# Two transformer blocks in float32: seven products in place of eight in parts of the gate and up layers, with adding DMAs

## The chip, the cores and the metric

One core of a Trainium2 chip runs the whole program. The metric is the device time of one execution in microseconds (us), and lower is better. The kernel before took 2581.62 us, the median of three runs (2581.48 to 2582.09).

## The reference

Two transformer blocks run one after the other on 256 tokens of width 2048, in float32. The first has window attention, gated linear attention and a feed forward layer; the second has latent attention, sparse attention, cross attention and a wide layer. The change is in the first block's feed forward layer, whose width is 5632:

```python
z = rmsnorm(h, norm_ffn_g[l])
ff = (jax.nn.silu(z @ w_ffn_gate[l]) * (z @ w_ffn_up[l])) @ w_ffn_down[l]
h = h + ff.astype(h.dtype)
```

## The kernel before

**Products.** TensorE multiplies in the type float32r, so that each float32 operand is held as the sum of a high part (the value rounded to float32r) and a low part (what is left), and each product of two tiles is three matmuls: high by high, high by low, low by high (`three` in `dense`, line 179, matmuls at L187). The activation's transposed parts (the class `Act`; zT for the gate and up layers, ffT for the down layer) lie in SBUF; they are the stationary operand, 128 rows of the inner dimension by 128 tokens. The weights stream from memory.

**Units.** A weight block of 256 rows by 512 columns, that is two row tiles, is a unit. `emit` (line 224) runs through the list of units. For each it calls `split` on a unit LEAD places ahead, then `load` on one still further ahead, then the unit's own matmuls. `load` issues the DMA into one of RAWB = 6 raw buffers on SP's queue (L232). `split` makes the high part with a ScalarE copy (L246) and the low part with a VectorE subtraction raw - high (L248); in a few units, those marked pool, GpSimd makes the low part. The parts go to LEAD + 1 rotating buffers called whi and wlo, with LEAD = 3. The split of unit n therefore writes buffers that an earlier unit's matmuls have to have finished reading. Each engine works through its instructions in the order in which the program issued them.

```python
nc.scalar.activation(out=hv, in_=r, func=AF.Copy)
eng = nc.gpsimd if u.pool else nc.vector
eng.tensor_tensor(out=l[:, : u.kn, : u.cn], in0=r, in1=hv.bitcast(F32), op=ALU.subtract)
```

**The feed forward layer.** It goes in three parts of 4, 4 and 3 chunks of 512 columns. For each chunk, `dense` puts eight units of the gate's weights into the program and eight of the up's, each unit with 12 matmuls (two row tiles, two token tiles, three matmuls). After the gate's units `evac_gate` (line 852) takes silu from PSUM on ScalarE (L858); after the up's, `evac_up` (line 871) multiplies on VectorE (L877). `ff_tr` transposes the result on TensorE (L289) into ffT one and two units later, with `hilo` splitting it on ScalarE (L277) and VectorE (L278). After each part four chunks of the down product follow, added to the residual by `evac_down` (L885). zT itself is written by `residual` (line 810) during the output product `w_out` before the gate: `make_h1` adds on VectorE (L845), `square_sum` squares on ScalarE (L308), and `to_act` transposes and splits with the gain (L295, L280, L281).

**Memory.** PSUM's eight banks are two accumulators of two banks and four rotating banks for the rest. SBUF is handed out by hand as 12 pages of 8 KB, 8 halves of 4 KB and 8 small pieces a partition.

**The end.** `last_chunk` does one half of the tokens after the other (matmuls at L1352); the parts of its first units are kept in pages, four of its eight with LEAD = 3, and every second low part there is made by GpSimd.

Of the kernel before, what the change touches and what calls it, by code (L numbers as in the profile page):

```python
# [19 lines left out]
LEAD = 3  # L20
RAWB = 6
NPAGE = 12
NHALF = 8
NBIT = 8
# [8 lines left out]
class Act:  # L33
    """A feature-major operand of a product, as the sum of two float32r parts."""
# [18 lines left out]

class Unit:
# [5 lines left out]
    def __init__(self, src, kn, cn, mm, pool=False, keep=False):  # L60
        self.src, self.kn, self.cn, self.mm, self.pool, self.keep = src, kn, cn, mm, pool, keep
# [3 lines left out]
def kernel(  # L65
# [18 lines left out]
    psa = ctx.enter_context(tc.tile_pool(name="psa", bufs=2, space=PS))  # L84
    pss = ctx.enter_context(tc.tile_pool(name="pss", bufs=4, space=PS))
# [10 lines left out]
    def take(lst, pool, name, shape, dt):  # L96
        if not lst:
            raise RuntimeError(f"no room for {name}: {sorted((v[1], v[3]) for v in owner.values())}")
# [8 lines left out]

    def half(name, shape, dt=F32):
        return take(free_h, halves, name, shape, dt) if free_h else page(name, shape, dt)
# [4 lines left out]
    def free(*ts):  # L114
        for t in ts:
            if isinstance(t, Act):
                free(*t.pages)
            else:
                lst, tag = owner.pop(id(t))[:2]
                lst.append(tag)  # L120
# [18 lines left out]

    def bank(name, shape):  # L140
        return pss.tile(shape, F32, tag="ps", name=name)

# [11 lines left out]
    def dense(W, c0, cn, kts, act, jobs, k_off=0, ka=0, src=None, pool=None, first=True, last=True, hold=None, groups=None, evac=None):  # L154
        """Appends the units of act^T-by-W products.

        jobs: ("N", off, n, b) tokens-by-columns products or ("T", off, n, b) columns-by-tokens
        ones, b the bank of the accumulator they go to (None: a bank for each half of the tokens).
        """
        hold = {} if hold is None else hold  # L160
        k0 = 0
        for kn in groups or [KG] * (kts // KG):
# [3 lines left out]
            else:  # L166
                s = src(k0, kn)

            def mm(hi, lo, k0=k0, kn=kn):
                if k0 == 0 and first:  # L170
                    hold["acc"] = psa.tile([P, 2, 512], F32, tag="acc", name="acc")
# [39 lines left out]

    after = {}
# [4 lines left out]
    def sched(u, *steps):  # L217
        """Puts closures behind units: (gap, fn) comes gap units after the one before it."""
# [5 lines left out]
    def emit(start):  # L224
        us = [e for kind, e in prog if kind == "U"]
        raws, spl = {}, {}

        def load(i):
            if i < len(us):
                r = wraw.tile([P, KG, 512], F32, tag="raw", name="raw")  # L230
                for dst, ap in us[i].src:
                    nc.sync.dma_start(dst(r), ap)  # L232
                raws[i] = r

        def split(i):
            if i < len(us):
                u = us[i]
                r = raws.pop(i)[:, : u.kn, : u.cn]
# [6 lines left out]
                hv = h[:, : u.kn, : u.cn]  # L245
                nc.scalar.activation(out=hv, in_=r, func=AF.Copy)  # L246
                eng = nc.gpsimd if u.pool else nc.vector
                eng.tensor_tensor(out=l[:, : u.kn, : u.cn], in0=r, in1=hv.bitcast(F32), op=ALU.subtract)  # L248
                spl[i] = (h, l)

        start(load, split)
        for j in range(LEAD):
            if j > 1:
                split(j)
            load(j + RAWB)
        i = 0
        for kind, e in prog:
# [4 lines left out]
            load(i + LEAD + RAWB)  # L262
# [20 lines left out]
    def to_act(src, dst, k, gain=None):  # L283
        """dst's row tiles k, k+1 from src(t, k), a [tokens, 128] block of half t."""
# [12 lines left out]

    def to_T(src, dst):
        """dst [128, 2, 256] (SBUF) from src(t, a)."""
# [10 lines left out]
    def rstd(ss, n, dst):  # L310
        """dst = (ss / n + eps) ** -0.5"""
# [5 lines left out]
    def bcast_a(r, scale=1.0):  # L317
        """With bcast_b(dst): dst [128, 256] is r ([tokens, 2]) along the free axis, on every partition."""
# [22 lines left out]
    junk = ctx.enter_context(tc.tile_pool(name="junk", bufs=2))  # L341
# [196 lines left out]
    def prep_kva():  # L538
        """Keys and values with the tokens of each half in reverse order."""
# [270 lines left out]
    def residual(name_T, gain, ssname, make):  # L810
        """The closure for chunk j of a residual update: make(j, t, acc) writes h[t]'s columns."""
        def evac(j):
            def fn(acc):
                if j == 0:
                    env[ssname] = small(ssname, [P, 2, 4])
                    env[name_T] = new_act(name_T, 16)
                if "h" not in env:
# [6 lines left out]
                for a in range(2):  # L824
                    k = 4 * j + 2 * a
                    later(2 + a, lambda k=k: to_act(lambda t, kk: h[t][:, kk * P : (kk + 1) * P], env[name_T], k, gain))
# [22 lines left out]
    res_h1 = residual("zT", G_FFN, "ssh1", make_h1)  # L849
# [742 lines left out]
```

## Time and profile before

| what | value |
|---|---|
| runs | 2581.48, 2581.62, 2582.09 us (median 2581.62) |
| profiled execution, first to last instruction (span) | 2579.6 us; no other time is listed for it |
| TensorE busy | 2561.9 us (99%) in 12464 instructions |
| VectorE busy | 1435.2 us (56%) |
| ScalarE busy | 1175.3 us (46%) |
| GpSimd busy | 65.7 us (3%) |
| mean granted TensorE clock | 0.999 |

In the profile, PE is TensorE's matmuls, PEld its weight loads, DVE VectorE, ACT ScalarE, POOL GpSimd and SP the engine that issues most DMAs. A busy time is what an engine spent inside instructions. Matmuls are pipelined, so that two of them overlap in the records, and the step from one to the next is the number that counts. The idle time of an engine has behind it in brackets what ended it. L187 is line 187 of the kernel.

### The profile page before, as it was taken

Reading aid. Unit: us, or ns where it says so; the run is one execution under the profiler, and the core shown is the slowest. Engines: PE = TensorE matmul, PEld = TensorE weight load, DVE = VectorE, ACT = ScalarE, POOL = GpSimd, SP = SyncE. Lnnn points to the kernel's source line nnn. Section 1 sums busy time; section 2 is a strip of 40 time slices with the busy share of each in tenths; the row PEclk is TensorE's granted clock in tenths of the full one; section 3 lists DMA queues with packets and bytes.
Section 4 is the critical chain, followed back from the end, with each engine's and each line's share of the span. In section 5 each row is a group of like instructions: output and inputs, shape, how many; then the busy total and the mean of one; then the engine's idle time right before and its main releaser. Section 6 shows DMA issues by size and latency. Waiting matters only on the chain.

```text
span 2579.6 us, 32028 instructions
## 1 busy us (share of the span) xinstructions
PE 2561.9 (99%) x12464; PEld 2146.7 (83%) x12464; DVE 1435.2 (56%) x1651; ACT 1175.3 (46%) x1562; POOL 65.7 (3%) x69
## 2 busy tenths in 40 slices
PE   8999999999999999999999999999999999999998
PEld 7898788888888888888889978889888888888886
DVE  5755465555455445555566658565655555455554
ACT  5545344444444344434455444464544443443443
POOL 1000000000000000000000000000100000000002
PEclk9999999999999999999999999999999999999999
DMA  7455566656665666566655734554665656656653
GB/s 254 155 166 173 154 212 189 188 188 187 189 188 193 191 191 190 189 210 190 191 170 170 203 115 151 187 180 139 189 193 189 193 183 193 190 185 209 187 187 129
DMA packets 259544, 472.77 MB, mean 183 GB/s; under 512 B 19402, under 2 KB 48848, under 8 KB 259136
## 3 DMA queue, kind: packets, MB, share of 16 engines
q1 hardware_dynamic: 256816, 461.76, 58.7%
q0 software_dynamic: 2544, 8.96, 1.0%
q8 instruction: 97, 1.59, 0.2%
q14 instruction: 55, 0.45, 0.0%
q10 hardware_dynamic: 32, 0.01, 0.0%
HBM read 468.55 MB, written 2.12 MB: 182 GB/s over the span
## 4 chain that ended last, share of the span: by engine, by line
PE 98%; issue 0%; ACT 0%; DMA 0%; POOL 0%; DVE 0%; SPq 0%; POOLq 0%; ACTq 0%
PE acc L187 92%; PE pt L289 1%; PE pt L295 1%; PE ptr L479 0%; PE po L499 0%; PE sc L1057 0%; PE ptT L303 0%; DMA raw<-in_w_in_dram 0%; PE sc L1056 0%; PE psi L1127 0%; PE sc L566 0%; PE po L494 0%; POOL wlo L248 0%; PE sc L1199 0%; ACT whi L246 0%
## 5 line engine op out<-in xcount | busy, mean ns | idle before, releaser
L248 DVE TENSOR_TENSOR wlo<-raw,whi 128x1024 fp32r<-128x1024 f32 (+5 forms) x889 | 1062.4, 1200 | 826.8 <-ACT whi L246 822.3
L246 ACT ACTIVATE whi<-raw 128x1024 fp32r<-128x1024 f32 (+5 forms) x895 | 921.6, 1033 | 903.6 <-PE acc L187 888.8
L187 PE MATMUL acc<-whi,ffTh 128*128 128x512 f32 x832 | 325.6, 391 | 0.0
L187 PE MATMUL acc<-whi,ffTl 128*128 128x512 f32 x832 | 324.0, 389 | 0.0
L187 PE MATMUL acc<-wlo,ffTh 128*128 128x512 f32 x832 | 323.7, 389 | 0.0
L187 PE MATMUL acc<-whi,zTh 128*128 128x512 f32 x704 | 275.7, 392 | 0.0
L187 PE MATMUL acc<-whi,zTl 128*128 128x512 f32 x704 | 274.2, 389 | 0.0
L187 PE MATMUL acc<-wlo,zTh 128*128 128x512 f32 x704 | 273.9, 389 | 0.0
L187 PE MATMUL acc<-whi,x4Th 128*128 128x512 f32 x512 | 201.9, 394 | 0.0
L187 PE MATMUL acc<-whi,uTh 128*128 128x512 f32 (+2 forms) x512 | 198.9, 388 | 2.4 <-ACT whi L246 1.8
L187 PE MATMUL acc<-whi,x4Tl 128*128 128x512 f32 x512 | 199.7, 390 | 0.0
L187 PE MATMUL acc<-wlo,x4Th 128*128 128x512 f32 x512 | 199.3, 389 | 0.0
L187 PE MATMUL acc<-whi,uTl 128*128 128x512 f32 (+2 forms) x512 | 193.9, 379 | 0.6 <-DVE uTl L281 0.6
L187 PE MATMUL acc<-wlo,uTh 128*128 128x512 f32 (+2 forms) x512 | 193.7, 378 | 0.0
L187 PEld LDWEIGHTS acc<-whi,ffTl 128*128 128x128 f32 x832 | 156.2, 188 | 32.8
L187 PEld LDWEIGHTS acc<-wlo,ffTh 128*128 128x128 f32 x832 | 156.3, 188 | 31.9
L187 PEld LDWEIGHTS acc<-whi,ffTh 128*128 128x128 f32 x832 | 156.2, 188 | 31.8
L187 PEld LDWEIGHTS acc<-whi,zTl 128*128 128x128 f32 x704 | 132.1, 188 | 27.8
L187 PEld LDWEIGHTS acc<-wlo,zTh 128*128 128x128 f32 x704 | 132.2, 188 | 27.0
L187 PEld LDWEIGHTS acc<-whi,zTh 128*128 128x128 f32 x704 | 132.2, 188 | 26.8
L187 PE MATMUL acc<-whi,u2Th 128*128 128x512 f32 (+2 forms) x352 | 132.6, 377 | 0.0
L187 PE MATMUL acc<-whi,u2Tl 128*128 128x512 f32 (+2 forms) x352 | 129.0, 366 | 0.0
(446 smaller groups left out, 3353.9 us busy)
## 6 DMA issues: line engine op xcount, KB each, us to landing
raw<-in_w_in_dram SPq DMA_DIRECT2D x167, 512.0 KB, 4.1
raw<-in_w_up_dram SPq DMA_DIRECT2D x128, 512.0 KB, 3.8
raw<-in_w_down_dram SPq DMA_DIRECT2D x128, 512.0 KB, 4.6
raw<-in_w_ffn_gate_dram SPq DMA_DIRECT2D x88, 512.0 KB, 4.4
raw<-in_w_ffn_up_dram SPq DMA_DIRECT2D x88, 512.0 KB, 3.8
raw<-in_w_ffn_down_dram SPq DMA_DIRECT2D x88, 512.0 KB, 4.2
raw<-in_w_out_dram SPq DMA_DIRECT2D x64, 512.0 KB, 4.3
raw<-in_w_in_dram SPq DMA_DIRECT2D x24, 368.0 KB, 3.3
```

The costliest lines, as they stand in the source:

```text
L187: nc.tensor.matmul(dst, lhsT=v if tr else u, rhs=u if tr else v, start=st, stop=end and j == 2, skip_group_check=True,)
L246: nc.scalar.activation(out=hv, in_=r, func=AF.Copy)
L248: eng.tensor_tensor(out=l[:, : u.kn, : u.cn], in0=r, in1=hv.bitcast(F32), op=ALU.subtract)
L289: nc.tensor.transpose(pt[:, a, t * P : (t + 1) * P], src(t, k + a), ident)
L295: nc.tensor.transpose(pt[:, t * P : (t + 1) * P], src(t, k + a), ident)
```

## The change

**Seven products.** `dense2` takes the gate's and the up's units of a chunk together. With two token tiles (rows), a pair of row tiles of the weights (inner) and gate and up (columns), the product of a pair is a 2 by 2 by 2 block product, eight tile products. In pairs marked S (three of the eight, by `kinds_z = "SCCSCSCC"`) seven products of sums of tiles stand in for the eight; in pairs marked C there are eight, into four of the seven accumulators. Each product is three matmuls as before. An S pair is four units: x (two products), u (two), v (two) and y (one); a C pair is two units of four products each. A chunk is 22 units. The sums of weights are made in `split` by three VectorE instructions of an S pair. The sums of activations are made once, in `to_act_sums`, while zT is written.

**Accumulators.** The seven accumulators take seven of PSUM's eight banks; the eighth holds the transposes meanwhile. `early` reads three of the seven after the third S pair; `finish` reads the other four with five additions at the chunk's end, and then `evac_gu` does silu and the multiplication from SBUF. The transposes follow 4 and 6 units later (3 and 4 in a part's last chunk).

**Adding DMA.** In C pairs that follow a C pair (the third and the eighth of a chunk, four units) VectorE makes no low part: ScalarE writes minus the high part into wlo, and an accumulating DMA on GpSimd's queue adds raw to it.

**Room.** LEAD goes from 3 to 4; two more buffers (wsum) hold sums of weights; halves go from 8 to 6, small pieces from 8 to 5, the buffers of `junk` from 2 to 1. When the halves run out, a page is now cut in two. `load_more` loads as many units ahead as there are raw buffers. The diff's core (the definition of `three` in `dense2` is the same three matmuls):

```diff
-LEAD = 3
+LEAD = 4
-NHALF = 8
-NBIT = 8
+NHALF = 6
+NBIT = 5
...
+    wsum = ctx.enter_context(tc.tile_pool(name="wsum", bufs=2))
...
+    def new_seven():
+        rot[:] = [7]
+        at = {1: 0, 3: 1, 5: 4, 7: 5, 6: 6, 4: 2, 2: 3}
+        return {i: psum.tile([P, 512], F32, tag=f"b{b}", name="acc") for i, b in at.items()}
...
+            if kinds[p] == "S":
+                qd = Quad()
+                fin = p == last_s
+                def mx(hi, lo, p=p, q=q, sm_=sm_, fin=fin):
+                    if p == 0:
+                        begin()
+                    three(1, q(0, 0), (hi[:, 0], lo[:, 0]), fin)
+                    three(3, sm_(3), (hi[:, 1], lo[:, 1]))
+                def mu(hi, lo, sm_=sm_, fin=fin):
+                    three(5, sm_(0), (hi[:, 0], lo[:, 0]))
+                    three(7, sm_(2), (hi[:, 1], lo[:, 1]), fin)
+                def mv(hi, lo, q=q, sm_=sm_, fin=fin):
+                    three(6, sm_(1), (hi[:, 0], lo[:, 0]), fin)
+                    three(4, q(1, 1), (hi[:, 1], lo[:, 1]))
+                    if fin:
+                        hold["c"] = early(hold["g"])
+                def my(hi, lo, q=q):
+                    three(2, q(0, 1), (hi[:, 0], lo[:, 0]))
+                x = [(lambda r: r[:, 0:1], blk(Wb, cb, k)), (lambda r: r[:, 1:2], blk(Wa, ca, k + 1))]
+                y = [(lambda r: r[:, 0:1], blk(Wa, ca, k)), (lambda r: r[:, 1:2], blk(Wb, cb, k + 1))]
+                for src, kn, mm, part in (([x, y], 2, mx, "x"), ([], 2, mu, "u"), ([], 2, mv, "v"), ([], 1, my, "y")):
+                    prog.append(("U", Unit(src, kn, 512, mm, quad=qd, part=part)))
...
+                def ma(hi, lo, q=q, sm_=sm_, end=end):
+                    for i in range(2):
+                        three(5, q(1, i), (hi[:, i], lo[:, i]), end and i == 1)
+                    for i in range(2):
+                        three(3, sm_(i), (hi[:, i], lo[:, i]), end and i == 1)
+                def mb(hi, lo, q=q, end=end):
+                    for i in range(2):
+                        three(2, q(0, i), (hi[:, i], lo[:, i]), end and i == 1)
+                    for i in range(2):
+                        three(4, q(1, i), (hi[:, i], lo[:, i]), end and i == 1)
+                for W, c, mm in ((Wa, ca, ma), (Wb, cb, mb)):
+                    prog.append(("U", Unit([[(lambda r: r, blk(W, c, k, 2))]], 2, 512, mm, add=kinds[p - 1] == "C")))
+        def early(g):
+            c = [half("c0", [P, 2, 512]), half("c1", [P, 2, 512])]
+            nc.scalar.activation(out=c[0][:, 1], in_=g[1], func=AF.Copy)
+            nc.vector.tensor_tensor(out=c[0][:, 0], in0=c[0][:, 1], in1=g[6], op=ALU.add)
+            nc.vector.tensor_tensor(out=c[1][:, 1], in0=c[0][:, 0], in1=g[7], op=ALU.add)
+            return c
+        def finish():
+            g, c = hold["g"], hold["c"]
+            add = lambda out, a, i: nc.vector.tensor_tensor(out=out, in0=a, in1=g[i], op=ALU.add)
+            add(c[0][:, 0], c[0][:, 0], 5)
+            add(c[0][:, 0], c[0][:, 0], 3)
+            add(c[1][:, 0], c[1][:, 1], 5)
+            add(c[0][:, 1], c[0][:, 1], 2)
+            add(c[1][:, 1], c[1][:, 1], 4)
+            evac(c)
+        F(finish)
...
+        def load_more():
+            while ahead["next"] < len(us) and ahead["raw"] + len(us[ahead["next"]].src) <= RAWB:
+                load(ahead["next"])
...
+                elif u.part == "x":
+                    q.x, q.y = got
+                    q.u = wsum.tile([P, 2, 512], F32, tag="sum", name="wu")
+                    q.v = wsum.tile([P, 2, 512], F32, tag="sum", name="wv")
+                    nc.vector.tensor_tensor(out=q.u, in0=q.x, in1=q.y[:, 0:1].to_broadcast([P, 2, 512]), op=ALU.subtract)
+                    r = q.x
+                elif u.part == "y":
+                    r = q.y[:, 1:2]
+                else:
+                    r, gone = (q.u if u.part == "u" else q.v), 0
...
+                if u.add:
+                    lv = l[:, : u.kn, : u.cn]
+                    nc.scalar.activation(out=lv, in_=r, func=AF.Copy, scale=-1.0)
+                    nc.gpsimd.dma_start(lv, r.bitcast(F32R), accum_op=ALU.add)
+                    nc.scalar.activation(out=hv, in_=r, func=AF.Copy)
+                    spl[i] = (h, l)
+                    ahead["raw"] -= gone
+                    return
                 nc.scalar.activation(out=hv, in_=r, func=AF.Copy)
                 eng = nc.gpsimd if u.pool else nc.vector
                 eng.tensor_tensor(out=l[:, : u.kn, : u.cn], in0=r, in1=hv.bitcast(F32), op=ALU.subtract)
+                if u.part == "x":
+                    nc.vector.tensor_tensor(out=q.v[:, 0], in0=q.x[:, 1], in1=q.u[:, 0], op=ALU.add)
+                    nc.vector.tensor_tensor(out=q.v[:, 1], in0=q.y[:, 1], in1=q.v[:, 0], op=ALU.subtract)
                 spl[i] = (h, l)
+                ahead["raw"] -= gone
...
+    def to_act_sums(src, dst, sums, k, gain):
+        f = half("f", [P, 4, S])
+        pt = bank("pt", [P, 2, S])
+        for a in range(2):
+            for t in range(2):
+                nc.tensor.transpose(pt[:, a, t * P : (t + 1) * P], src(t, k + a), ident)
+        for a in range(2):
+            nc.scalar.activation(out=f[:, a], in_=pt[:, a], func=AF.Copy, scale=gains[:, gain + k + a : gain + k + a + 1])
+        hilo(f[:, 0:2], dst.hi(k, 2), dst.lo(k, 2))
+        a1, a2 = f[:, 0:2, :P], f[:, 0:2, P:]
+        h, l = sums.parts(k // 2)
+        if sums.kinds[k // 2] == "S":
+            v = f[:, 2:4].rearrange("p a (b s) -> p (a b) s", b=2)
+            stt = nc.vector.scalar_tensor_tensor
+            stt(out=v[:, 0], in0=a2[:, 0], scalar=-1.0, in1=a2[:, 1], op0=ALU.mult, op1=ALU.subtract)
+            nc.vector.tensor_sub(out=v[:, 2], in0=a1[:, 0], in1=a2[:, 0])
+            stt(out=v[:, 1], in0=v[:, 0], scalar=-1.0, in1=a1[:, 0], op0=ALU.mult, op1=ALU.subtract)
+            nc.vector.tensor_sub(out=v[:, 3], in0=a1[:, 1], in1=v[:, 1])
+        else:
+            v = f[:, 2].rearrange("p (b s) -> p b s", b=2)
+            nc.vector.tensor_sub(out=v, in0=a1, in1=a2)
+        hilo(v, h, l)
+        free(f)
...
+                        later(2 + a, lambda k=k: to_act_sums(src, env[name_T], env[name_T + "s"], k, gain))
...
+    kinds_z = "SCCSCSCC"
+    res_h1 = residual("zT", G_FFN, "ssh1", make_h1, kinds_z)
...
+            later(lag + gap * a, tr(a))
...
+        def fn(c):
+            if first:
+                env["r"] = rnorm("ssh1", 16)
             if j == 0:
                 env["ffT"] = new_act("ffT", 4 * n)
-            sg = env["sg"]
             for t in range(2):
-                nc.vector.scalar_tensor_tensor(out=sg[:, t], in0=acc[:, t], scalar=env["r"][:, t : t + 1], in1=sg[:, t], op0=ALU.mult, op1=ALU.mult)
-            ff_tr(sg, j, 1)
+                nc.scalar.activation(out=c[t][:, 0], in_=c[t][:, 0], func=AF.Silu, scale=env["r"][:, t : t + 1])
+            for t in range(2):
+                nc.vector.scalar_tensor_tensor(out=c[t][:, 0], in0=c[t][:, 1], scalar=env["r"][:, t : t + 1], in1=c[t][:, 0], op0=ALU.mult, op1=ALU.mult)
+            ff_tr(lambda t: c[t][:, 0], j, 4 if j < n - 1 else 3, 2 if j < n - 1 else 1, c)
...
             o = (c0 + j) * 512
-            dense(w_ffn_gate[0], o, 512, 16, A("zT"), full, evac=evac_gate(j if i == 0 else 9))
-            dense(w_ffn_up[0], o, 512, 16, A("zT"), full, evac=evac_up(j, n))
+            dense2(w_ffn_gate[0], o, w_ffn_up[0], o, 16, A("zT"), zsums, kinds_z, evac_gu(j, n, i == 0 and j == 0))
```

## Rows read from the trace of the kernel before

**Rows 1.** The page: busy time by engine; the chain that ended last.

```profile
PE 2561.9 (99%) x12464; PEld 2146.7 (83%) x12464; DVE 1435.2 (56%) x1651; ACT 1175.3 (46%) x1562; POOL 65.7 (3%) x69
...
PE 98%; issue 0%; ACT 0%; DMA 0%; POOL 0%; DVE 0%; SPq 0%; POOLq 0%; ACTq 0%
PE acc L187 92%; PE pt L289 1%; PE pt L295 1%; PE ptr L479 0%; PE po L499 0%; PE sc L1057 0%; PE ptT L303 0%; DMA raw<-in_w_in_dram 0%; PE sc L1056 0%; PE psi L1127 0%; PE sc L566 0%; PE po L494 0%; POOL wlo L248 0%; PE sc L1199 0%; ACT whi L246 0%
```

**Rows 2.** The chain in order of time, one chunk: start, length (us), what.

```profile
675.49 40.85 PE acc L187 x180
716.35 0.44 PE pt L289 x4
...
719.97 10.23 PE acc L187 x45
```

**Rows 3.** Windows: stretch, length, busy time by engine, granted clock, DMA share, GB/s.

```profile
573.00:624.00 51.00, 51.00 (x234) 42.23 (x233) 28.07 (x31) 24.24 (x34) 0.00 (x0) 1.00 0.59 186
...
624.30:802.20 177.90, 177.90 (x802) 147.26 (x801) 89.65 (x84) 79.18 (x87) 3.72 (x5) 1.00 0.65 190
...
329.00:347.00 18.00, 18.00 (x84) 14.89 (x82) 16.56 (x25) 8.76 (x11) 4.98 (x5) 1.00 0.68 229
```

**Rows 4.** VectorE's and ScalarE's groups, 624.3 to 802.2: busy us, mean ns, idle before.

```profile
L248 DVE TENSOR_TENSOR wlo<-raw,whi 128x1024 fp32r<-128x1024 f32 x64 | 78.3, 1225 | 78.4 <-ACT whi L246 78.4
L877 DVE SCALAR_TENSOR_TENSOR sg<-acc,st,sg 128x512 f32<-128x512 f32 x6 | 4.2, 747 | 1.3 <-PE acc L187 1.3
L278 DVE TENSOR_TENSOR ffTl<-pt,ffTh 128x512 fp32r<-128x512 f32 x6 | 4.2, 692 | 6.8 <-ACT ffTh L277 6.8
...
L246 ACT ACTIVATE whi<-raw 128x1024 fp32r<-128x1024 f32 x64 | 67.6, 1059 | 75.3 <-PE acc L187 75.3
L858 ACT ACTIVATE sg<-acc,st 128x512 f32<-128x512 f32 x8 | 5.1, 686 | 5.0 <-PE acc L187 5.0
L277 ACT ACTIVATE ffTh<-pt 128x512 fp32r<-128x512 f32 x6 | 3.6, 599 | 11.3 <-PE pt L289 11.3
L280 ACT ACTIVATE zTh<-pt,gains 128x256 fp32r<-128x256 f32 x4 | 1.7, 470 | 3.1 <-PE pt L295 3.1
L858 ACT ACT_TABLE_LOAD x1 | 1.3, 1283 | 1.7 <-PE acc L187 1.7
```

**Rows 5.** Timeline of VectorE: start, length of the merged instructions, how many.

```profile
559.57 2.36 DVE L248 TENSOR_TENSOR wlo<-raw,whi 128x1024 fp32r<-128x1024 f32 x2 [1.76 <-ACT whi L246]
...
624.69 1.28 DVE L845 TENSOR_TENSOR h<-xr,acc 128x512 f32<-128x512 f32 x2 [0.40 <-PE acc L187]
```

**Rows 6.** The tile xr: its DMA on GpSimd's queue (issue, ns), and landing.

```profile
L839 POOL DMA_DIRECT2D xr<-in_x_dram x4: 722/726/781, 335.0 to 342.4; - x4
...
DMA to landing us min/median/max: 4.8/5.4/6.2
```

**Rows 7.** Timeline of GpSimd.

```profile
334.96 1.51 POOL L839 DMA_DIRECT2D xr<-in_x_dram  x2
...
647.37 0.72 POOL L315 TENSOR_TENSOR st<-var,mhalf 128x2 f32<-128x2 f32 x1 [304.21 <-DVE var L314]
...
1666.94 2.94 POOL L1227 DMA_DIRECT2D mem<-in_mem_dram  x4 [65.26 <-PE po L499]
```

**Rows 8.** The tile mem: landing of its four DMAs.

```profile
DMA to landing us min/median/max: 4.5/6.4/8.7
```

**Rows 9.** Timeline of ScalarE at the first gate chunk, which begins at 624.3.

```profile
626.04 0.62 ACT L308 ACTIVATE junk<-h 128x512 f32<-128x512 f32 x1
...
626.65 1.99 ACT L246 ACTIVATE whi<-raw 128x1024 fp32r<-128x1024 f32 x2
```

**Rows 10.** Timeline of TensorE in the last chunk: its three waits.

```profile
2551.59 0.50 PE L1352 MATMUL acc<-kept,ffTh 128*128 128x512 f32 x1 [1.26 <-POOL kept L248]
...
2554.93 0.50 PE L1352 MATMUL acc<-wlo,ffTh 128*128 128x512 f32 x1 [0.28 <-POOL wlo L248]
...
2558.25 0.50 PE L1352 MATMUL acc<-wlo,ffTh 128*128 128x512 f32 x1 [0.32 <-POOL wlo L248]
```

**Rows 11.** The page: a gate load, KB and us to landing.

```profile
raw<-in_w_ffn_gate_dram SPq DMA_DIRECT2D x88, 512.0 KB, 4.4
```

More of the change, by code (lines that the diff above doesn't have):

```diff
@@ L51, in lo, with __init__, parts, __getitem__ @@
         return self.part(self.l, k, n)
+class Sums:
+    def __init__(self, kinds, new):
+        self.kinds, self.pages, self.at, last = kinds, [], [], None
+        for i, kind in enumerate(kinds):
+            if kind == "S":
+                t = new(f"sum{i}")
+                self.pages.append(t)
+                self.at.append((t, 0, 4))
+            elif last is None:
+                last = new(f"sum{i}")
+                self.pages.append(last)
+                self.at.append((last, 0, 2))
+            else:
+                self.at.append((last, 4, 2))
+                last = None
+    def parts(self, p):
+        t, o, n = self.at[p]
+        return t[:, o : o + n], t[:, o + n : o + 2 * n]
+class Acc:
+    def __init__(self, tiles):
+        self.tiles = tiles
+    def __getitem__(self, key):
+        return self.tiles[key[1]][(key[0], *(key[2:] or (slice(None),)))]
+class Quad:
+    pass
 class Unit:
-    def __init__(self, src, kn, cn, mm, pool=False, keep=False):
-        self.src, self.kn, self.cn, self.mm, self.pool, self.keep = src, kn, cn, mm, pool, keep
+    def __init__(self, src, kn, cn, mm, pool=False, keep=False, quad=None, part=None, add=False):
+        self.add = add
+        self.src, self.kn, self.cn, self.mm, self.pool, self.keep, self.quad, self.part = src, kn, cn, mm, pool, keep, quad, part
 @with_exitstack
@@ L106, in page @@
         return take(free_p, pages, name, shape, dt)
+    split_pages = []
     def half(name, shape, dt=F32):
-        return take(free_h, halves, name, shape, dt) if free_h else page(name, shape, dt)
+        if free_h:
+            return take(free_h, halves, name, shape, dt)
+        for sp in split_pages:
+            if sp["free"]:
+                break
+        else:
+            sp = {"page": page(name, [P, 2, 1024]), "free": [0, 1]}
+            split_pages.append(sp)
+        i, n = sp["free"].pop(0), 1
+        for m in shape[1:]:
+            n *= m
+        v = sp["page"][:, i, :n]
+        if dt is not F32:
+            v = v.bitcast(dt)
+        if len(shape) > 2:
+            names = "abcde"[: len(shape) - 1]
+            v = v.rearrange(f"p ({' '.join(names)}) -> p {' '.join(names)}", **dict(zip(names, shape[1:])))
+        v = v[: shape[0]]
+        owner[id(v)] = (sp, i, v, name)
+        return v
     def bit(name, shape, dt=F32):
@@ L210, in dense, with dense2, blk, three @@
         return hold
+    def dense2(Wa, ca, Wb, cb, kts, act, sums, kinds, evac):
+        n, hold, last_s = kts // 2, {}, max(i for i, k in enumerate(kinds) if k == "S")
+        assert kinds[0] == "S" and kinds[n - 1] == "C"
+        def blk(W, c, k, m=1):
+            return W[k * P : (k + m) * P, c : c + 512].rearrange("(k p) f -> p k f", p=P)
+        def three(i, a, w, stop=False):
+            g = hold["g"][i]
+            st = i not in hold["seen"]
+            hold["seen"].add(i)
+            for j, (u, v) in enumerate(((a[0], w[0]), (a[0], w[1]), (a[1], w[0]))):
+                nc.tensor.matmul(g, lhsT=u, rhs=v, start=st and j == 0, stop=stop and j == 2, skip_group_check=True)
+        def begin():
+            hold["g"], hold["seen"] = new_seven(), set()
+        for p in range(n):
+            k = 2 * p
+            def q(t, i, k=k):
+                tok, a = slice(t * P, (t + 1) * P), act()
+                return a.hi(k + i)[:, 0, tok], a.lo(k + i)[:, 0, tok]
+            def sm_(i, p=p):
+                h, l = sums().parts(p)
+                return h[:, i], l[:, i]
+            if kinds[p] == "S":
[20 more added lines that the diff above has]
+                    prog.append(("U", Unit(src, kn, 512, mm, quad=qd, part=part)))
+            else:
+                end = p == n - 1
+                def ma(hi, lo, q=q, sm_=sm_, end=end):
[26 more added lines that the diff above has]
+        F(finish)
@@ L254, in emit @@
                 split(j)
-            load(j + RAWB)
+            load_more()
         i = 0
@@ L261, in emit @@
             split(i + LEAD)
-            load(i + LEAD + RAWB)
+            load_more()
             e.mm(*spl.pop(i))
@@ L807, in evac_pb, with residual @@
         return fn
-    def residual(name_T, gain, ssname, make):
+    def residual(name_T, gain, ssname, make, kinds=None):
         def evac(j):
```

87 lines of the change are left out of this document (54 added, 33 removed).

## The prediction

> **What bounds the kernel now.** I read the page first: TensorE is busy 99% of the span and is 98% of the chain that ended last, 92% of it in the products at L187 [rows 1]. So time goes only with matmuls, or with waits that appear between them. The chain in order of time gives the price of a matmul: 180 of them in 40.85 us, 0.227 us each, with nothing between; four transposes take 0.44 us [rows 2]. A unit of 12 is 2.72 us. The windows show the gate and up stage: in 177.9 us VectorE works 89.7, ScalarE 79.2, GpSimd almost nothing, and the DMA engines are at 0.65 [rows 3]. VectorE's 64 low parts have as much idle time before them as work, and wait for ScalarE's high parts; those in turn wait for TensorE to free a buffer [rows 4]. The side engines have slack, TensorE has none. Only a wait that outlasts this slack costs time.
>
> **What it removes.** An S pair has 7 x 3 = 21 matmuls in place of 24. Three pairs in each of 11 chunks: 99 matmuls x 0.227 = 22.5 us, all on the path. A chunk shrinks from 192 to 183 matmuls, 43.5 to 41.5 us. Every matmul keeps its shape, so I keep the price.
>
> **What it adds on VectorE.** Back to back, two subtractions of 1024 columns take 2.36 us, 1.13 apart [rows 5]; two of 512 columns take 1.28, 0.60 apart [rows 5]. An S pair needs the sum u (1.13), two sums v (1.2), three low parts of 1024 (3.4) and one of 512 (0.6): 6.3 us beside 4.8 us of TensorE. A C pair needs 2.3 beside 5.4, or nothing where the DMA adds. Seven additions (4.2), two multiplications at 0.75 and two low parts of ffT at 0.69 [rows 4] add 7.1. The sum is 3 x 6.3 + 3 x 2.3 + 7.1 = 33 us of a chunk of 41.5 + 0.9 for transposes: not a bound in the mean. What counts is where it is late.
>
> **Three places where it could be late.** I followed the order of the program through a chunk, its start at 0. S units last 1.36, 1.36, 1.36 and 0.68 us; LEAD = 4 lets unit n be split from the start of unit n-4, 0.2 us after which ScalarE begins.
> (a) After an S pair, unit n-4 to n is only 4.8 us; the high part (1.06) and low part (1.23) take 2.5. VectorE comes out of the S pair about when it must start the next C unit, and is 2.3 us early.
> (b) The chunk's end. VectorE finishes unit y of the next chunk at 40.2, then five additions, done at 43.2. The next chunk starts at 41.5 on an accumulator read long before, and needs the second one at 42.2; the addition that frees it ends at 41.4. Silu ends on ScalarE at 42.7, the multiplications at 44.5, the low part of the next chunk's unit 4 at 45.8; TensorE needs it at 46.5. Margin 0.7 in both. I cost it at zero; it is 0.7 from costing something.
> (c) The adding DMAs. For units 20 and 21, ScalarE's minus copies end at 29.8 and 32.5, the parts are needed at 36.3 and 39.0. For units 6 and 7 the copies come after silu, and the room is the same: 6.5 us from copy to matmul, for issue and landing.
>
> **The adding DMA** is in no row. The nearest is a plain DMA on the same queue with the same 512 KB to 128 partitions: it lands 5.4 us after issue, 4.8 to 6.2, its issue taking 0.73 [rows 6]. These were issued in pairs 0.75 us apart [rows 7], with VectorE busy 16.6 of 18 us around them [rows 3], so VectorE did not hold up the issue. The other bound is two plain DMAs in place of one, as it reads two operands: four of 512 KB within 2.94 us [rows 7] land 4.5 to 8.7 after issue [rows 8]. By the first the cost is nothing. By the second, units 20 and 21 are like those four, and the second lands 2.2 us late, in each of 22 pairs: 48 us. I take the first as it is nearest in size, queue and spacing, and as both ends here lie in SBUF, with no read of memory; I keep the second.
>
> The Trainium skill speaks for the second: Collectives: The Full Stack, "The bandwidth ceiling: the fold count and why AG ≠ RS ≠ AR", says that in the DMA engines it is not the addition that costs but its two source reads, which halve the rate. No row here can show it; by it the time would be the 2612 of the first rival.
>
> **One-time costs.** In the first chunk the transposes and sums of zT's last two pairs run in its first units. ScalarE starts unit 4's high part 2.35 us in, after the squares, as now [rows 9]; then come two scaled copies at 0.47, a high part at 0.6 and one of the sums for each pair, with a wait for VectorE's sum. With one bank for transposes the second set waits 0.8. Unit 6's minus copy ends at about 8.3, unit 7's at 13.3; landing 5.4 later they are 1.6 and 2.2 late. At its end silu waits for the norm (GpSimd's power, 0.72 [rows 7]) and perhaps a table load of 1.28 [rows 4]: 1.4 to 2.7 late, take 2. Together 6.6 us; between 0 and 10.
>
> **The tail.** Three kept units in place of four, and one more unit of lead, let GpSimd's and VectorE's low parts for the last chunk be issued before the squares. TensorE waits there 1.26 + 0.28 + 0.32 for GpSimd [rows 10]: 1.9 us back, at worst none.
>
> **Other edits.** The sums of zT load the output product's stage, where in 51 us VectorE works 28 and ScalarE 24 [rows 3]. A pair of row tiles costs VectorE at most six instructions of at most 0.60 [rows 5], 3.6 us, two pairs in a chunk of eight units, 21.8 us, with ten such idle: hidden behind the lead, four units or 10.9 us; without that cover it would be 3.6 a pair. SP issues four pieces of 256 KB for an S pair in place of two; a gate load lands after 4.4 us [rows 11], and raw buffers come free some two pairs, over 8 us, before they are needed: nothing, until the adding DMAs hold raw longer than 7 us. Fewer halves may make a write wait for a late reader. No row prices it; I bound it by two units of 2.72, 5.4 us, and take 0.
>
> **Sum.** -22.5 - 1.9 + 6.6 = -17.8. On the profiled span, 2579.6 (the median of the runs is 2.0 longer): 2561.8. On the median: 2564.
>
> **Rivals.**
> 1. *The adding DMA lands too late* (the other side). Behind the minus copy it has 6.5 us. What decides is its landing: at 7.3 us a wait of 0.8 in each of 22 pairs eats the 17.8; at 8.7 it is 48 us, so 2612. For it: two reads, and DMA engines that are at 0.65 already, or 0.68 with the shorter chunk, with 4 x 512 KB more on 16 x 512 KB, a quarter more or, doubled, half: 0.85 to 1.0. Against: the plain DMA [rows 6], with 1.1 us to spare, at a share as high.
> 2. *VectorE becomes the bound* at the chunk's end, where the margin is 0.7 and several short instructions each pass a semaphore. If the chain there is 1.7 longer, it costs 1 us a chunk, 11 us: 2575. For it: VectorE has hardly a gap from 31 to 45. Against: the mean of 33 in 42.
> 3. *No gain to measure*: waits of about 0.8 a pair between the two cases, or several small ones. 2577 to 2587.
>
> **How the numbers follow.** A measurement of this kernel can tell 0.2%, about 5.2 us: faster is below 2576.4, slower above 2586.8. Forecast (2556 to 2572) 0.55, rival 2 0.12, rival 3 0.09, rival 1 0.24. Faster 0.55 + 0.12 = 0.67. The forecast's own range is the sum without one-time costs and with them at 10, plus 5 for halves: 2557 to 2572. The range for 8 in 10 leaves out the half of rival 1 in which landing nears 8.7, and goes from 2556 to 2606.
>
> **What would show it.** Right: the products in the gate and up stage go from 2112 to 2013; the chain shows 183 matmuls a chunk at 0.227 with no waits for the DMA; adding DMAs land 5 to 6.5 us after issue; the chunk's pitch falls from 44.5 to 42.4; the three waits in the tail are gone; waits only in the first chunk. Wrong: a wait of TensorE for the DMA into wlo of 1 to 2 us twice a chunk (rival 1), or for VectorE's additions or the low part of unit 4 (rival 2); matmuls further apart than 0.227 in S pairs would break the price itself.

## The result, and the profile after

The changed kernel takes 2601.31 us, the median of four runs (2597.84 to 2601.97), against 2581.72 before in the same series: 1.0073 times as long (interval 1.0059 to 1.0087), 19.6 us slower. I had forecast 2564, 17.8 us faster. The profiled execution took 2601.97 us, with a span of 2600.2.

The page of the changed kernel: busy time, the software queue (packets, MB, share of 16 engines), the chain by engine and the adding DMA's line. They answer to [rows 1] and [rows 11].

```profile
PE 2555.8 (98%) x12365; PEld 2130.0 (82%) x12365; DVE 1568.7 (60%) x1866; ACT 1285.4 (49%) x1699; POOL 102.2 (4%) x113
...
q0 software_dynamic: 8880, 32.03, 5.6%
...
PE 84%; DMA 7%; issue 4%; ACT 2%; DVE 2%; SPq 0%; POOL 0%; ACTq 0%; POOLq 0%; DVEq 0%
...
wlo<-raw POOLq DMA_DIRECT2D x44, 512.0 KB, 7.4
```

The 99 matmuls are gone (12464 to 12365), and yet the chain, 98% TensorE before, now lies 7% in DMAs. TensorE's waits name them; the columns are the sum in us, how many, and the longest:

```profile
PE acc L318 <- DMA wlo<-raw: 23.1, 24, 3.5
PE acc L274 <- ACT uTh L503: 3.7, 1, 3.7
...
PEld acc L318 <- DMA wlo<-raw: 35.7, 35, 3.9
```

No DMA line stood in TensorE's waits before, and the wait for uTh was 0.7. L318 is what L187 was in the new products; matmuls and weight loads overlap, so the two DMA lines are not added (the 59 us of waits in the expectations below is that sum; TensorE's own is 23.1). The second line is another loss, at the program's start, 600 us ahead of the changed layer.

The windows of the first gate and up part (columns as in [rows 3]), of 100 us within it, and of the flight of one pair of adding DMAs:

```profile
633.00:820.00 187.00, 173.30 (x748) 139.04 (x748) 131.81 (x150) 111.17 (x126) 14.62 (x17) 0.98 0.79 222
...
690.00:790.00 100.00, 93.84 (x410) 75.59 (x409) 75.49 (x85) 59.37 (x67) 6.88 (x8) 0.98 0.82 230
...
761.40:772.00 10.60, 9.98 (x44) 7.89 (x44) 7.39 (x8) 6.51 (x8) 1.72 (x2) 1.00 0.96 245
```

TensorE is no longer filled: 93.8 of 100 us. VectorE is busy 75 of 100, not the bound. The DMA share rose from 0.65 to 0.8, and to 0.96 while a pair flies. The chain in order of time shows one such flight, and GpSimd's timeline the issue of its pair:

```profile
761.43 7.11 DMA wlo<-raw
768.54 0.04 issue
768.58 2.84 PE acc L318 x11
```

```profile
761.43 0.86 POOL L460 DMA_DIRECT2D wlo<-raw  x1 [25.65 <-ACT wlo L459]
763.81 0.86 POOL L460 DMA_DIRECT2D wlo<-raw  x1 [1.52 <-ACT wlo L459]
```

The minus copy released the issue at 761.43, the DMA landed 7.11 us later, and the matmul began at 768.58 after a wait of 0.62. So the room, from issue to the matmul's due time (767.96), was 6.5 us, as I had worked out. The landing is what differed. The tile wlo, over all 44, answers to [rows 6]:

```profile
DMA to landing us min/median/max: 4.8/7.4/9.6
```

The waits cost more than themselves. TensorE's timeline around one of the longest, and the windows' row of what follows it (the number behind the engines' busy times is the granted clock):

```profile
695.24 0.50 PE L318 MATMUL acc<-wlo,zTh 128*128 128x512 f32 x1 [3.25 <-DMA wlo<-raw]
...
696.49 0.63 PE L318 MATMUL acc<-whi,zTl 128*128 128x512 f32 x1
696.92 0.63 PE L318 MATMUL acc<-whi,sum 128*128 128x512 f32 x1
...
699.46 0.39 PE L318 MATMUL acc<-whi,zTh 128*128 128x512 f32 x1
```

```profile
696.00:699.00 3.00, 3.00 (x8) 2.31 (x8) 0.90 (x1) 0.00 (x0) 0.00 (x0) 0.50 0.71 198
```

Eight matmuls run 0.43 us apart in place of 0.227, at a granted clock of 0.50, the lower of its two levels (1.2 GHz): 1.6 us more. There are three such stretches in the changed layer, after the waits of 3.46, 3.25 and 2.89 us, and one at the start. The short waits, too, cost more than the figure in brackets:

```profile
767.58 0.39 PE L318 MATMUL acc<-whi,zTh 128*128 128x512 f32 x1
768.58 0.50 PE L318 MATMUL acc<-wlo,zTh 128*128 128x512 f32 x1 [0.62 <-DMA wlo<-raw]
768.92 0.40 PE L318 MATMUL acc<-whi,zTl 128*128 128x512 f32 x1
```

From start to start these are 1.00 and 0.34 us, 0.89 more than two steps of 0.227, for a wait listed as 0.62. By an estimate from this row, some 0.27 us more for each of the 24 waits, with the 23.1 listed and three times 1.6, the stage loses about 34 us.

### The profile page after: what moved, and what is told of

Its sections match the earlier page's. It is cut to its first block, busy times and chain, and to the rows that moved or that the text cites. A ratio compares the mean times of both kernels' runs of the same rounds, so it can differ in the third digit from the quotient of the medians.

```text
span 2600.2 us, 32596 instructions
## 1 busy us (share of the span) xinstructions
PE 2555.8 (98%) x12365; PEld 2130.0 (82%) x12365; DVE 1568.7 (60%) x1866; ACT 1285.4 (49%) x1699; POOL 102.2 (4%) x113
## 4 chain that ended last, share of the span: by engine, by line
PE 84%; DMA 7%; issue 4%; ACT 2%; DVE 2%; SPq 0%; POOL 0%; ACTq 0%; POOLq 0%; DVEq 0%
PE acc L274 72%; PE acc L318 6%; DMA wlo<-raw 5%; DMA raw<-in_w_ffn_gate_dram 1%; ACT whi L465 1%; DVE wlo L467 1%; PE pt L512 1%; PE pt L518 1%; ACT wlo L459 1%; PE ptr L727 0%; DVE c L389 0%; PE acc L1602 0%; PE po L747 0%; ACT whi L461 0%; DMA raw<-in_w_in_dram 0%
## 5 line engine op out<-in xcount | busy, mean ns | idle before, releaser
L467 DVE TENSOR_TENSOR wlo<-raw,whi 128x1024 fp32r<-128x1024 f32 (+5 forms) x845 | 988.3, 1176 | 719.2 <-ACT whi L465 713.3
L465 ACT ACTIVATE whi<-raw 128x1024 fp32r<-128x1024 f32 (+5 forms) x852 | 859.0, 1014 | 775.0 <-PE acc L274 661.3
L274 PE MATMUL acc<-whi,ffTh 128*128 128x512 f32 x864 | 333.4, 392 | 0.9 <-DVE c L389 0.9
L274 PE MATMUL acc<-whi,ffTl 128*128 128x512 f32 x800 | 311.6, 389 | 0.0
L318 PE MATMUL acc<-wlo,zTh 128*128 128x512 f32 x429 | 172.0, 401 | 23.8 <-DMA wlo<-raw 23.1
L318 PE MATMUL acc<-whi,zTh 128*128 128x512 f32 x429 | 169.5, 395 | 0.0
L318 PE MATMUL acc<-whi,zTl 128*128 128x512 f32 x429 | 168.4, 393 | 0.0
L318 PE MATMUL acc<-whi,sum 128*128 128x512 f32 x484 | 165.6, 394 | 0.9 <-DVE c L389 0.9
L274 PE MATMUL acc<-wlo,u2Th 128*128 128x512 f32 (+2 forms) x352 | 128.8, 366 | 0.0
L318 PEld LDWEIGHTS acc<-wlo,zTh 128*128 128x128 f32 x429 | 81.0, 189 | 52.2 <-DMA wlo<-raw 35.7
```

The costliest lines, as they stand in the source:

```text
L274: nc.tensor.matmul(dst, lhsT=v if tr else u, rhs=u if tr else v, start=st, stop=end and j == 2, skip_group_check=True,)
L318: nc.tensor.matmul(g, lhsT=u, rhs=v, start=st and j == 0, stop=stop and j == 2, skip_group_check=True)
```

## The experiments

Each edit is against the changed kernel unless it says so. Times are medians; "before" was between 2581.47 and 2581.65 in each series.

### Is it the wait, the addition, or the traffic?

**Plain copies.** The DMA copies raw over the minus part and adds nothing.

```diff
-                    nc.gpsimd.dma_start(lv, r.bitcast(F32R), accum_op=ALU.add)
+                    nc.gpsimd.dma_start(lv, r.bitcast(F32R))
```

> The accumulating DMA becomes a plain copy of raw into wlo: same queue, size and places, no addition (so wlo holds raw, not the low part). Theory A, the addition's second read makes the landing long (7.4 us in the changed kernel, room 6.5): landing falls to 5 to 6 us, TensorE's waits for wlo from 59 us to under 15, time 2570 to 2580. Theory B, it is the queue, the size and the loads beside it: landing stays at 7 us or more, time 2595 to 2602.

**No adding DMA.** VectorE makes all low parts.

```diff
-... mm, add=kinds[p - 1] == "C")))
+... mm, add=False)))
```

> VectorE makes all low parts; no adding DMA. Theory A, the late landings are nearly all of the loss and VectorE is only full at a chunk's end: its 2.3 us more there cost about 1.7 us a chunk, so 2575 to 2585. Theory C, VectorE is the bound whatever the DMA does: 2600 or more. If VectorE had room for them after all: 2562 to 2570.

**DMAs that nobody waits for.** They are issued as before; TensorE uses the high part in the low part's place.

```diff
-                    spl[i] = (h, l)
+                    spl[i] = (h, h)
```

> The adding DMAs are issued as in the change, but the products of these units read the high part in place of the low part (so this part of the result is left out), and TensorE doesn't wait for the landing; raw and wlo buffers still do. Theory A: the stalls in the gate and up stage go, 2563 to 2572. Theory D, the DMA traffic itself (loads late, DMA engines near full) costs as much as the wait: 2585 or more.

| kernel | us (runs from to) | against before | landing, median | queue q0 |
|---|---|---|---|---|
| changed | 2601.31 (2597.84 to 2601.97) | 1.0073 [1.0059, 1.0087] | 7.4 | 5.6% |
| plain copies | 2574.59 (2573.18 to 2576.63) | 0.9974 [0.9963, 0.9985] | 5.9 | 3.5% |
| nobody waits | 2573.80 (2571.78 to 2576.66) | 0.9969 [0.9958, 0.9980] | 7.5 | 5.6% |
| no adding DMA | 2569.91 (2569.73 to 2570.83) | 0.9955 [0.9941, 0.9970] | none | 1.1% |

The wait is the loss: without it the same 44 DMAs, landing as late, leave the kernel 27.5 us faster. That is 1.8 above theory A's range; TensorE's waits there are for VectorE's additions, 4.3 and 2.9 us. The addition makes the landing late: plain copies of the same size at the same places land in 5.9, inside the room of 6.5, and give back 26.7. Their landing, and the software queue of the plain copies and of the kernel with no adding DMA:

```profile
DMA to landing us min/median/max: 3.9/5.9/7.2
...
q0 software_dynamic: 8880, 32.03, 3.5%
...
q0 software_dynamic: 2544, 8.96, 1.1%
```

The 3.9 us from the kernel where nobody waits to the one without these DMAs is not the price of the traffic as such: issued earlier (below), the same 44 adding DMAs leave a kernel of 2569.93 us. What it is was not taken apart. The 100 us of the windows, where nobody waits: TensorE full at a DMA share of 0.85.

```profile
690.00:790.00 100.00, 100.00 (x450) 82.80 (x449) 80.61 (x90) 64.27 (x72) 6.87 (x8) 1.00 0.85 253
```

By an estimate from the queue's share, an adding DMA takes (5.6 - 1.1)% x 2600 / 44 = 2.7 us of all 16 engines, a plain one (3.5 - 1.1)% x 2575 / 44 = 1.4. The Trainium skill's Collectives: The Full Stack ("The bandwidth ceiling: the fold count and why AG ≠ RS ≠ AR") gives a factor of two for an addition's two source reads, in a ReduceScatter beside an AllGather. The engines' time here agrees (2.7 against 1.4), while the landing grows by a quarter only (7.4 against 5.9).

My expectation for the kernel without adding DMAs was too high: VectorE had the room for all low parts. Its chain of waits around one chunk, its waits, and the same 100 us in the windows:

```profile
720.92 0.44 PE pt L512 x4
...
727.29 36.08 PE acc L318 x159
763.37 0.44 PE pt L512 x4
```

```profile
PE acc L318 <- DVE c L389: 3.4, 2, 2.6
...
PE acc L274 <- DVE c L389: 1.2, 3, 0.4
```

```profile
690.00:790.00 100.00, 100.00 (x450) 82.77 (x449) 88.67 (x96) 58.10 (x65) 0.00 (x0) 1.00 0.63 196
```

From one chunk's transposes to the next there are 42.45 us, which is the 42.4 of the forecast, at 36.08 / 159 = 0.227 a matmul. VectorE is busy 89 of 100 us, and in all eleven chunks together TensorE waits twice for its additions, 3.4 us, and three times, 1.2 us, where a down product follows.

### The start

> For the first eight units the split four ahead is issued behind the unit's products and transposes, not in front. Theory: one more high part in front of uT's on ScalarE is what delays the start by 3.9 us (TensorE waits 3.7 for uTh, then runs at half clock): 3 to 5 us less than the changed kernel, 2596 to 2598. Rival: the start is late by chance of the first loads: no change beyond 1 us.

```diff
-            split(i + LEAD)
-            load_more()
+            if i >= 8:
+                split(i + LEAD)
+                load_more()
             e.mm(*spl.pop(i))
             for fn in after.pop(i, ()):
                 fn()
+            if i < 8:
+                split(i + LEAD)
+                load_more()
```

2596.39 us (2594.03 to 2598.76), 4.9 less than the changed kernel. The changed kernel's timelines of TensorE and ScalarE there, and then the wait for uTh in this kernel and in the one before:

```profile
15.89 0.50 PE L274 MATMUL acc<-whi,uTh 128*128 128x512 f32 x1 [3.73 <-ACT uTh L503]
...
18.20 0.63 PE L274 MATMUL acc<-wlo,uTh 128*128 128x512 f32 x1
```

```profile
14.42 1.06 ACT L465 ACTIVATE whi<-raw 128x1024 fp32r<-128x1024 f32 x1 [1.62 <-DMA raw<-in_w_in_dram]
15.38 0.82 ACT L503 ACTIVATE uTh<-pt,gains 128x256 fp32r<-128x256 f32 x2
```

```profile
PE acc L274 <- ACT uTh L507: 1.6, 1, 1.6
...
PE acc L187 <- ACT uTh L280: 0.7, 1, 0.7
```

With LEAD = 4 ScalarE has one more unit's high part in its queue ahead of uTh, which TensorE needs. That high part waits 1.62 for its own load, and uTh stands behind it; TensorE's wait is 3.73 in place of 0.7, and a stretch at half the clock follows it. The edit moves the loads behind the matmuls together with the splits, and which of the two counts was not run apart; the trace names the high part. The same edit brought 3.5 to 6.3 us in the four other pairs of kernels below that differ by it alone.

### One adding DMA of each pair

```diff
-... add=kinds[p - 1] == "C")))
+... add=kinds[p - 1] == "C" and W is Wa)))
```

> Only the first unit of a pair that follows a C pair (the gate's) has its low part from the adding DMA, the second has it from VectorE: 22 adding DMAs in place of 44, no two of them 2 us apart any more. Theory A, the two DMAs of a pair are in each other's way (each takes about 2.7 us of all 16 engines, beside the loads): a single one lands at 6.5 us or under, TensorE's waits for wlo fall from 59 us to under 12, and the time is 2574 to 2580 us. Theory B, each adding DMA is late by itself: the landing stays at about 7.4 us, half of the waits stay (25 to 30 us), and the time is 2584 to 2589 us.

2595.76 us (2591.80 to 2599.70). The tile wlo and the waits:

```profile
DMA to landing us min/median/max: 4.9/7.2/8.8
```

```profile
PE acc L318 <- DMA wlo<-raw: 18.0, 17, 3.6
...
PEld acc L318 <- DMA wlo<-raw: 26.6, 22, 3.9
```

Theory A falls: alone, a DMA lands about as late (7.2). Theory B had the landing, but not the waits: of the 59 us (both lines added) it let half stay, and 18.0 + 26.6 = 44.6 stayed, so its time was 7 us too low. Half of the DMAs cost 25.9 us (to 2569.91) where all cost 31.4: the first of a pair makes TensorE late, and the second then lands partly in time. In the changed kernel's timeline the first ones account for 16.9 of the 23.1 us of waits (16 waits among 22), the second ones for 6.2 (8 waits).

### More room

The minus copy and the DMA go out n units earlier, into buffers of their own; the high part stays where it was. Core of the edit, in `emit`:

```diff
             split(i + LEAD)
+            add_lo(i + LEAD + n)
             load_more()
...
+        def add_lo(i):
+            if i < len(us) and us[i].add:
+                l = early_lo[i] = half("lo", [P, KG, 512], F32R)
+                r = raws[i][0]
+                nc.scalar.activation(out=l, in_=r, func=AF.Copy, scale=-1.0)
+                nc.gpsimd.dma_start(l, r.bitcast(F32R), accum_op=ALU.add)
```

One unit earlier (n = 1):

> The adding DMAs are as in the changed kernel, all 44, but ScalarE's minus copy and the DMA of a unit go out one unit (2.7 us) earlier, into a half of its own in place of a wlo buffer. Theory A, landing against room is the whole matter: 2.7 us more room against a landing of 7.4 (4.8 to 9.6) leaves waits for wlo of under 12 us in place of 59, and the time is 2575 to 2581 us, near the 2573.8 without any wait. Theory B, the DMAs cost by what they hold up (the loads, the raw buffers, GpSimd's queue), so an earlier issue only moves the wait: 2590 to 2602 us.

Two units earlier (n = 2):

> The same, two units (5.4 us) earlier. Theory A: no wait of TensorE for an adding DMA is left (the slowest landing is 9.6, the room about 11.9), and the time is 2572 to 2576 us. Theory B: 2590 to 2602 us, and TensorE waits for loads or buffers instead.

Two units earlier, with the start's edit from above:

> The same as the kernel with two units more room, and the first 8 units of the program issue their split ahead after their own matmuls. Theory A, the two repairs add up: 4 to 5 us less than the kernel with two units more room, 2567 to 2571 us, so that it ends 2 to 5 us above the 2565.7 of the kernel with no adding DMA and the same start (the price of the DMA traffic). Theory B, with the waits gone VectorE's spare time counts: at or under 2565 us.

They took 2597.11 (2595.03 to 2600.78), 2597.99 (2594.91 to 2599.15) and 2592.50 us (2590.09 to 2593.66): almost nothing came back. The first two lie in theory B's ranges and the third in neither; but TensorE still waited for the adding DMAs (18.0 and 18.5 us with n = 1 and 2), not for loads or buffers as theory B says. The traces showed that I had not done what I had written. GpSimd's timeline with n = 2, and the matmul that needs this unit:

```profile
662.46 0.85 POOL L478 DMA_DIRECT2D lo<-raw  x1 [26.03 <-ACT lo L477]
```

```profile
671.58 0.50 PE L318 MATMUL acc<-lo,zTh 128*128 128x512 f32 x1 [1.08 <-DMA lo<-raw]
```

671.58 - 1.08 - 662.46 = 8.0 us of room, not 11.9: the units skipped are short ones of an S pair, and the minus copy now stands behind a high part of 1.06 on ScalarE. With n = 1 it is 6.7 for the first of a pair. And the landing rose with it, to 7.6 and 8.7 in the median. Three units take in the whole S pair, so I went there, with all DMAs and with one of each pair (two buffers in one page, as n = 3 needs them longer):

> All 44 adding DMAs, their minus copies and issues three units earlier than in the changed kernel (buffers of their own, two in one page). The units skipped before were short: from issue to use there were 6.5 us in the changed kernel, 6.7 with one unit more and 8.0 with two, not 9.2 and 11.9 as I wrote; three units take in a whole S pair and a C unit, 2.72 + 4.76 + 5.44 - 2.3 = 10.6 us. Theory A, landing against room decides: the landing stays under 10.6 in nearly all, TensorE's waits for lo are under 10 us, and the time is 2573 to 2579 us. Theory B, the landing grows with the room again, as it did from 7.4 to 8.7 (the DMA engines are near 1.0 while it flies), so waits of 30 us or more stay: 2588 to 2600 us.

> One adding DMA of each pair (22), issued three units earlier. Theory A: landing about 7.2 against a room of 10.6, no wait for lo is left, 2570 to 2574 us (the kernel with no adding DMA took 2569.9). Theory B: the landing grows with the room, waits of 20 us or more stay, 2585 to 2596 us.

2569.93 (2569.36 to 2571.51) and 2569.94 us (2568.69 to 2570.22). With all 44, the tile lo and the windows' row of one flight:

```profile
DMA to landing us min/median/max: 5.0/6.6/10.8
```

```profile
743.40:751.00 7.60, 7.60 (x35) 6.28 (x34) 5.72 (x7) 6.40 (x8) 1.66 (x2) 1.00 0.90 222
```

The weight loads wait for these DMAs 0.8 us in all, and the time is 3 us under theory A's range, at a DMA share of 0.90 in this flight. The landing is shorter, but that alone would not do: with a median of 6.6, more than half of the 44 land later than the 6.5 us of the changed kernel's room. One of them, by GpSimd's timeline, the tile lo in 745 to 747 us, and TensorE's timeline at the unit that reads it:

```profile
745.63 0.86 POOL L481 DMA_DIRECT2D lo<-raw  x1 [1.42 <-ACT lo L480]
```

```profile
DMA to landing us min/median/max: 9.2/9.2/9.2
```

```profile
756.22 0.39 PE L318 MATMUL acc<-lo,zTh 128*128 128x512 f32 x1
```

The room is 756.22 - 745.63 = 10.6, as forecast, and a landing of 9.2 costs nothing. So theory A holds: landing against room is the matter, and theory B falls. Why the landing was 8.7 with n = 2 and 6.6 with n = 3 is not settled; the share while they flew (0.90 to 0.97 in four windows over three flights with n = 3, 0.87 to 0.98 in six with n = 2) hardly tells them apart.

### Versions that beat both kernels

All have the start's edit. With no adding DMA:

> VectorE makes all low parts (no adding DMA), and the first 8 units of the program issue their split ahead after their own matmuls instead of before, as with a lead of 3 in effect at the start. The rest is the changed kernel. Theory A, what the start lost (3.7 us of wait for uTh and a stretch at half the clock) is independent of the gate stage: 2569.9 - 4.9 = 2565 us, no wait over 2 us for uTh. Theory B, the start's loss is taken up later by another wait: 2568 to 2570 us.

With no adding DMA and `kinds_z = "SCSCSCCC"`:

> No adding DMA, the start mended, and the three S pairs at places 1, 3 and 5 of the eight in place of 1, 4 and 6, so that VectorE has three C pairs (16 us) at the end of a chunk to catch up. Theory A, the waits that are left without the adding DMA (3.4 us for the additions, 2.5 us at the first chunk's end) come from VectorE being late at the chunk's end: they go, and the time is 2558 to 2563 us. Theory B, they come from one-time work in a part's first chunk, which the order of pairs doesn't change: within 2 us of the kernel with the old order, 2563 to 2567 us.

With no adding DMA and `kinds_z = "SCCSCCCC"`:

> No adding DMA, the start mended, and two S pairs in a chunk (places 1 and 4) in place of three. Against the kernel with three S pairs in the order 1, 3, 5 TensorE has 33 matmuls more, 33 x 0.227 = 7.5 us. Theory A, VectorE costs next to nothing with three: this one is 5 to 9 us slower, 2566 to 2572 us. Theory B, the third S pair is paid for by waits for VectorE: the two come out within 3 us of each other.

With 44 and with 22 adding DMAs, three units earlier:

> The 44 adding DMAs with three units more room, and the first 8 units of the program issue their split ahead after their own matmuls. The two repairs don't touch each other: 2569.9 - 4.5 = 2565 to 2566 us, the wait for uTh under 2 us. If VectorE's spare time (DVE 46 us less busy than without adding DMAs) is worth anything, 2563 us or less.

> The same with one adding DMA of each pair: 2565 us. If the DMA traffic costs by itself, 1 to 2 us less than with 44; if VectorE's spare time counts, as much more.

| kernel, with the start mended | us (runs from to) | against before |
|---|---|---|
| no adding DMA | 2565.74 (2564.22 to 2566.07) | 0.9938 [0.9925, 0.9950] |
| no adding DMA, S at 1, 3, 5 | 2569.66 (2569.40 to 2570.06) | 0.9954 [0.9940, 0.9968] |
| no adding DMA, two S pairs | 2567.83 (2567.75 to 2567.92) | 0.9947 [0.9934, 0.9959] |
| 44, three units earlier | 2566.41 (2566.10 to 2567.09) | 0.9941 [0.9929, 0.9954] |
| 22, three units earlier | 2563.65 (2563.50 to 2565.93) | 0.9932 [0.9919, 0.9946] |

The order S at 1, 3, 5 was my mistake, and both theories missed it. The waits name the place:

```profile
PE pt L516 <- DVE ffTl L505: 3.1, 8, 1.0
```

The transposes, not the accumulators, wait, eight times. My reading, which no run tests, is that S pairs close together at a chunk's start meet what VectorE owes the chunk before (additions, multiplications, ffTl). The order that stood was better.

The third S pair, worth 7.5 us of matmuls, brought 2.1 against two S pairs (2565.74 against 2567.83). Theory B of the run with two S pairs holds by its number, 1.8 us, but only because the order 1, 3, 5 was slow. Where the other 5.4 went, the kernel with three S pairs, no adding DMA and the start mended shows: TensorE waits twice for VectorE's additions at L318, 3.4 us in all, which the kernel with two S pairs does not. The longer of these waits, at the end of the third part's first chunk, has a stretch at half the clock behind it:

```profile
1187.16 0.50 PE L318 MATMUL acc<-whi,sum 128*128 128x512 f32 x1 [2.65 <-DVE c L389]
```

```profile
1188.20:1191.50 3.30, 3.30 (x9) 2.62 (x8) 3.30 (x6) 3.06 (x4) 0.00 (x0) 0.50 0.09 32
```

With its 1.6 us and 0.27 for each wait that is 5.5, so that the third S pair is paid for at one or two places, not in every chunk. Why VectorE is late there was not looked at.

Of the last two lines of the table the second is the best kernel measured, 0.7% faster than before. Its runs do not overlap with those of the kernel with 44 (2.8 us apart); with none they overlap, so that the gain of 22 over none is not shown.

## Why the prediction was wrong

The forecast was 2564, the result 2601.3: 37.3 us apart. The runs split it: 31.4 by the adding DMAs (2601.3 to 2569.9), 4.2 by the start (2569.9 to 2565.7), and 1.7 for all the rest of the sum, gains and losses together.

- **Removed matmuls: right.** 99 fewer, still 0.227 each, the pitch 42.45 where nothing waits for a DMA.
- **The adding DMA: the step that failed.** The room was worked out as 6.5 and was 6.5. Its landing I took at a plain DMA's 5.4 [rows 6], "as it is nearest in size, queue and spacing, and as both ends here lie in SBUF, with no read of memory". Between SBUF and SBUF a plain DMA landed in 5.9, not sooner than from memory, and the addition took it to 7.4. Of the 2.0 that were missing, 1.5 are the addition; 0.5 are the place or the fuller DMA engines, which no run separates. The row's DMAs flew at a DMA share of 0.68 [rows 3] and these at up to 0.96, where rival 1 itself had 0.85 to 1.0, so that "at a share as high" did not hold. The other bound, two plain DMAs, was the nearer one in kind.
- **Rival 1 is what happened,** and at its break-even: I had said that at 7.3 us a wait of 0.8 in each of 22 pairs eats the gain. At 7.4 the waiting cost 27.5 us, the distance to the kernel where nobody waits, 1.2 a pair. The median hides a spread of 4.8 to 9.6 in which only the late ones count, each wait cost some 0.27 more than its length, and three waits brought the half clock with them. I had a term for neither.
- **VectorE: right in the main.** Costed at nothing with margins of 0.7; even with all low parts its additions cost TensorE 3.4 + 1.2 us of waits, all in the third part and at the ends of parts, where rival 2 had 1 us in every chunk. The order 1, 3, 5 shows that rival 2 was near.
- **One-time costs: right in size.** The first two adding DMAs of the first chunk made TensorE wait 1.17 and 3.46 us, where I had 1.6 and 2.2. For the bank and silu I had 2.8; in the kernel with no adding DMA and the start mended, TensorE waits 0.3 and 0.6 us behind the first chunk. TensorE's timeline there, in the changed kernel:

```profile
641.20 0.50 PE L318 MATMUL acc<-wlo,zTh 128*128 128x512 f32 x1 [1.17 <-DMA wlo<-raw]
...
647.67 0.50 PE L318 MATMUL acc<-wlo,zTh 128*128 128x512 f32 x1 [3.46 <-DMA wlo<-raw]
```

- **The tail: right.** The three waits of [rows 10] have no successor in the last chunk.
- **Other edits: wrong in one.** LEAD = 4 was followed through the changed layer and the end, not to the program's start, where the edit that takes it back brought 3.5 to 6.3 us. It acts on every stage, and I looked at two.

Rival 3 is out: the two large terms, -24 and +31, are both far from nothing, and the small total hides them.

## What to carry to other kernels

For a DMA that adds, expect a later landing than a plain one's (7.4 against 5.9 here) and about twice the engines' time. Compare the late end of its landing, not its median, with the room from issue to use; the room is counted in the time of the units in between, not in their number. Where an engine off the critical path still has room, work moved away from it gains nothing (2569.93 against 2569.91 here). A wait moved onto TensorE costs its length, some 0.27 us more, and sometimes the half clock as well: in the changed kernel it followed the four waits of 2.9 to 3.7 us. In other runs it followed a wait of 1.85 (where nobody waits for the DMAs) and did not follow one of 2.80 (the start's edit), so a wait's length alone does not tell. A constant such as a lead acts everywhere: follow it through the program's start and end as well.

## What was not expected of the hardware

A 512 KB addition between two places in SBUF took 2.7 us of all 16 DMA engines (by the estimate above) and landed after 7.4 us, a plain copy there 1.4 and 5.9. Its issue held GpSimd 0.86 us, the plain copy's 0.53. Landing hardly went down when half of these DMAs were taken away (7.2). With the DMA engines at 0.85 over 100 us, TensorE still ran without a gap where it did not wait for the adding DMAs themselves.
